# Table buffers, store queues and the low parts of the gate matrices in a hybrid S5 / FNet kernel on Trainium2

## The chip, the cores and the metric

The kernel runs on one core of a Trainium2 chip. The metric is the device time of one execution in microseconds (us), the median over several runs. A core has five engines that run their own instruction lists and wait for each other by semaphores: PE (TensorE, matrix products; PEld is its weight load), DVE (VectorE), ACT (ScalarE), POOL (GpSimd) and SP (SyncE, which here only issues transfers). Transfers between the chip's main memory and the on-chip memory (DMA) are issued from the queue of an engine, here SP's or POOL's, in the order of the program.

## The reference

Two layers over 1024 latent tokens of width 1024, with 256 context tokens ahead of them. All the change lies in layer 0:

```
hl  = rmsnorm(xl) * (1 + scale) + shift                    # scale, shift, gate = silu(c) @ ada_w + ada_b
pl  = hl @ w_in ;  pc = hc @ w_in[:, :768]                 # 768 S5 + 256 FNet + 1024 gate columns
a   = exp(lam * step) ;  B' = ((a - 1) / lam) * B
s_t = a * s_(t-1) + B' u_t                                 # per group of 16 channels, 64 complex states, two directions
y   = Re(C s) + d * u
ya  = gelu(y) * sigmoid(gelu(y) @ glu_w + glu_b) ;  yb = fft2(u) @ f_w
xl  = xl + gate * (([ya, yb] * silu(z)) @ w_out)
```

Layer 1 (pooling, short convolution) and the last norm follow, and the change doesn't touch them.

## The kernel before

**Projections.** `w_in` comes in 16 blocks ("tiles" m) of 128 columns. Each is loaded into a buffer `raw` (four of them, tag `raw`), and split into a high part `whi` (ACT) and a low part `wlo` = raw − whi (DVE or POOL); one tile on PE is 48 matmuls 128x512: per k, high times high, high times low, low times high. `w_split(name)` makes the two parts, `w_take(name)` hands them out, and a `raw` buffer is free for the next load when `wlo` is done. The order of the loads is a fixed list (`w_init`): from tile 8 on it is win(m+1), then four blocks of `in_ada` that the 32 `adaps` matmuls behind tile m read straight from `raw` (`ada_part`).

**S5 tables.** In m = 0 to 5 (S5 columns) a function `fill()` is called from hooks inside the tiles: it makes the next of 24 tables on DVE and lets PE, ACT and the queues finish the table of two calls before. The first twelve (`bl_task`) are B' matrices: DVE writes `bl`, PE transposes it (`pt`), ACT copies the result to `bltw`, POOL's queue stores it in `bltd`. The other twelve (`cl_task`) are C matrices: DVE writes `cl`, which is stored in `cld` by two transfers; PE multiplies it (`pz`), ACT copies to `z`, DVE adds a diagonal (`dg`), and `z` is stored in `zd` for every second table. `cl` has two buffers and `z` has two. The queue for `cld` and `zd` is `self.sq`: SP's at first, POOL's from tile 6 on.

**B' u.** `bl_mm(i)`, i = 0 to 11, multiplies table i with the projected inputs `ub` (PE `vps`, ACT to `va` for i < 6 and `vb` for the rest). Both are loaded from main memory three calls ahead (`bl_load`). The first six calls lie in the hooks of tile 6 (`fx(0, hook0)`, output `fx`, stored in `xd`), the other six behind it. `vb` takes the place of the buffers of the table stage, so its first write waits for their last stores. The buffers `ut`, `utc`, `bltw`, `blt`, `ub`, `fx` share eight places (tag `slot`).

**Scan.** The scan over blocks of eight tokens is done by DVE: `tree(c, l)` over the context, c = 0 on `va`, c = 1 on `vb`; six single steps of `va` (SKEW); then 121 fused steps of six small operations each, kept in `bgq`, which `bg(n)` deals out. They are dealt in the hooks of tile 7 (`fx(1, ...)`) and of the gate tiles m = 8 to 15, so DVE scans while PE multiplies. The low parts of matrices 8 to 15 are made by POOL meanwhile. Behind the scan stands the y phase: `y_copy` (`sy`, ACT and DVE), `y_mm` (`yps`), `y_gelu`, then FNet, GLU, output, layer 1.

The program order is as written, with some reordering by a scheduler; each engine and each queue runs its own list in order.

Of the kernel before, what the change touches and what calls it, by code (L numbers as in the profile page):

```python
# [9 lines left out]
F32 = mybir.dt.float32  # L10
F32R = mybir.dt.float32r
I32 = mybir.dt.int32
AF = mybir.ActivationFunctionType
# [4 lines left out]
P = 128  # L18
# [176 lines left out]
class Builder:  # L195
# [218 lines left out]
    def s5_prelim(self, tp, s5s, raw):  # L414
# [88 lines left out]
                    self.act(self.acf[:, o[0], o[1]], pw[:, k, 8], scale=sc)  # L503
        return tables, inputs

    def bl_task(self, b, hf):

        nc = self.nc
        g4 = slice(8 * b + 4 * hf, 8 * b + 4 * hf + 4)
        bl = self.gt.tile([P, 2, 4, 16, 8], F32, tag="bl", name="bl", bufs=2)  # L510

        def dve():
            p = self.gt.tile([P, 4, 16, 8], F32, tag="blp", name="blp", bufs=1)
            B = [x[:, g4].unsqueeze(3).to_broadcast([P, 4, 16, 8]) for x in (self.bbs, self.bb[:, 0], self.bb[:, 1])]
            W = [self.pwb[:, i, g4].unsqueeze(2).to_broadcast([P, 4, 16, 8]) for i in range(3)]
            self.mul(p, B[0], W[0])
            self.mul(bl[:, 0], B[2], W[2])
            self.mul(bl[:, 1], B[1], W[1])
            self.sub(bl[:, 0], p, bl[:, 0])
            self.add(bl[:, 1], p, bl[:, 1])  # L520

        def pe():
            blt = self.slot("bltw").rearrange("p (r g n) -> p r g n", r=2, g=4)
            for ri in range(2):
                pt = self.ps("m", "pt")
                for g in range(4):
                    nc.tensor.transpose(pt[:, g * P:g * P + P], bl[:, ri, g].rearrange("p h s -> p (h s)"),  # L527
                                        self.c("ident"))
                self.act(blt[:, ri].rearrange("p g n -> p (g n)"), pt)
            nc.gpsimd.dma_start(self.bltd[b][:, :, 4 * hf:4 * hf + 4], blt)  # L530
        return dve, pe

    def cl_task(self, b, hf):
# [1 line left out]
        nc = self.nc  # L535
        g0 = 8 * b + 4 * hf
        g4 = slice(g0, g0 + 4)
        cl = self.kt.tile([P, 2, 4, 144], F32, tag="cl", name="cl", bufs=2)

        def dve():  # L540
            p = self.kt.tile([P, 4 * 144], F32, tag="clp", name="clp", bufs=1)
            p4 = p.rearrange("p (g e h) -> p g e h", g=4, e=9)
            C = [x[:, g4].unsqueeze(2).to_broadcast([P, 4, 9, 16]) for x in (self.cbs, self.cb[:, 0], self.cb[:, 1])]
            W = [self.pwc[:, i, :, g4].rearrange("p e g -> p g e").unsqueeze(3).to_broadcast([P, 4, 9, 16])
                 for i in range(3)]
            c4 = cl.rearrange("p r g (e h) -> p r g e h", e=9)
            self.mul(p4, C[0], W[0])
            self.mul(c4[:, 0], C[2], W[2])
            self.mul(c4[:, 1], C[1], W[1])
            self.sub(c4[:, 0], p4, c4[:, 0])  # L550
            cf = cl[:, 1].rearrange("p g e -> p (g e)")
            self.stt(cf, p, -1.0, cf, ALU.mult, ALU.subtract)
            for d in range(2):
                r = slice(64 * d, 64 * d + 64)
                o = 16 * (1 - d)
                self.sq.dma_start(self.cld[b][r, :, 4 * hf:4 * hf + 4], cl[r, :, :, o:o + 128])

        def pe():
            pz = [self.ps("m", "pz"), self.ps("m", "pz")]
# [188 lines left out]
    def layer0(self, es):  # L748
# [187 lines left out]
        for x in rest:  # L936
            if not isinstance(x, int):
                x()
        tables(0)
        inputs = inputs()  # L940
        for _ in range(4):
            next(inputs)


# [3 lines left out]
            return hh[k], hlo[k]  # L948

        todo = []  # L950
        for b in range(6):
            todo += [(self.bl_task, b, 0), (self.bl_task, b, 1)]
# [5 lines left out]
        self.sq = nc.sync  # L958

        def flush():  # L960
            for b, z in self.zq:
                self.sq.dma_start(self.zd[b].rearrange("a p e -> p a e"), z)
            self.zq = []

        def fill():
            flush()
            if len(pend) == 2 or not todo:
                if pend:
                    pend.pop(0)()
            if todo:  # L970
                f, b, hf = todo.pop(0)
                t = f(b, hf)
                if f == self.cl_task and b + hf == 0:
                    self.add(self.cbs, self.cb[:, 0], self.cb[:, 1])
                t[0]()
                pend.append(t[1])
# [2 lines left out]

        def bl_load(i):  # L980
            b, hf = divmod(i, 2)
            blt = self.slot("blt").rearrange("p (r g n) -> p r g n", r=2, g=4)
            nc.sync.dma_start(blt, self.bltd[b][:, :, 4 * hf:4 * hf + 4])
            ub = self.slot("ub")[:, 0:768].rearrange("p (g j) -> p g j", g=4)
            nc.sync.dma_start(ub, self.ud[b][4 * hf:4 * hf + 4].rearrange("g h s j -> (h s) g j"))
            blq.append((blt, ub))

        for m in range(6):
# [11 lines left out]
            if m == 1:  # L1000
                tables(1)
                sx.close()
                self.gt = ax.enter_context(tc.tile_pool(name="gt", bufs=1))
                self.kt = kx.enter_context(tc.tile_pool(name="kt", bufs=1, side="right"))
# [8 lines left out]
            self.mm3([(pc[:, :TC], 0, TC)], hi, lo, lambda k: (chh[k], chl[k]), 8)  # L1013
            if m == 0:
                self.w_split(names[2])
                for _ in inputs:
                    pass
            else:
                fill()
# [14 lines left out]
        def bl_mm(i):  # L1034
            blt, ub = blq.pop(0)
            for ri in range(2):
                for g0, n in ((0, 3), (3, 1)):
# [7 lines left out]
                    c, gl = divmod(4 * i + g0, NH)  # L1045
                    dst = v[c][:, :, ri, gl:gl + n].rearrange("p i g -> p g i")
                    src = ps[:, 0:160 * n].rearrange("p (g i) -> p g i", g=n)
                    self.act(dst, src)
            if i + 3 < 12:
                bl_load(i + 3)  # L1050

        blk = list(range(12))
        self.sq = nc.gpsimd

        def fx(ct, hook):
            x = self.slot("fx")
# [4 lines left out]
            return lambda: nc.gpsimd.dma_start(xd[:, ct], x)  # L1061

        def hook0(k):
            if k not in (2, 5):
                bl_mm(blk.pop(0))
                fill()

        fx(0, hook0)()
# [53 lines left out]
        while blk:  # L1122
            bl_mm(blk.pop(0))
            if len(blk) == 0:
                self.w_split(names[8], nc.gpsimd)
            if len(blk) < 5:
                tree(0, 4 - len(blk))
        for i in range(NC_, NC_ + SKEW):
# [7 lines left out]
        store = fx(1, lambda k: self.bg(2 if k % 4 else 1))  # L1136
        zt = [self.slot(f"zt{k}") for k in range(KD)]
        gates = [(0, ch) for ch in range(8, 12)] + [(1, ch) for ch in range(12)]
        for m in range(8, 16):
            k = m - 8  # L1140
            hl = self.w_take(names[m])
            if m < 15:
                self.w_split(names[m + 1], nc.gpsimd)
            if m == 8:
                store()
            self.proj(hl, hr, 8, lambda p, c0, c1: self.act(zt[k][:, c0:c1], p, AF.Silu),
                      hook=lambda k: self.bg(2 if k % 4 else 1))
# [678 lines left out]
```

## Time and profile before

| | before |
|---|---|
| time, median of 3 runs | 913.28 us (912.3 to 913.72) |
| the profiled execution: its time / its span | 915.5 us / 913.7 us |
| mean granted TensorE clock | 0.976 |
| busy in the span: PE, DVE, ACT, POOL | 95%, 74%, 38%, 10% |
| DMA moved | 129.16 MB, mean 141 GB/s |

Times in the rows are microseconds from the start of the span of the profiled execution, which is 2.2 us longer than the median of the other runs. A row of a timeline is: start, duration, engine, line, operation, output<-inputs, shape, count, and in brackets the idle time of the engine just before and what ended it. PE is near full almost everywhere; the stretches where it isn't are what a change of order can win.

### The profile page before, as it was taken

Reading aid. Unit: us, or ns where it says so; the run is one execution under the profiler, and the core shown is the slowest. Engines: PE = TensorE matmul, PEld = TensorE weight load, DVE = VectorE, ACT = ScalarE, POOL = GpSimd, SP = SyncE. Lnnn points to the kernel's source line nnn. Section 1 sums busy time; section 2 is a strip of 40 time slices with the busy share of each in tenths; the row PEclk is TensorE's granted clock in tenths of the full one; section 3 lists DMA queues with packets and bytes.
Section 4 is the critical chain, followed back from the end, with each engine's and each line's share of the span. In section 5 each row is a group of like instructions: output and inputs, shape, how many; then the busy total and the mean of one; then the engine's idle time right before and its main releaser. Section 6 shows DMA issues by size and latency. Waiting matters only on the chain.

```text
span 913.7 us, 14101 instructions
## 1 busy us (share of the span) xinstructions
PE 864.6 (95%) x5312; PEld 708.2 (78%) x5312; DVE 673.0 (74%) x1740; ACT 343.4 (38%) x597; POOL 94.2 (10%) x91
## 2 busy tenths in 40 slices
PE   9997998989999967799999999999999999999995
PEld 4666886768777747787888999877778888878995
DVE  7777997857999996755457376698887776785354
ACT  4547341446112109843433143542222333263111
POOL 0002321221221212300016001000000000000000
PEclk9899999999999988999999999999999999999997
DMA  9642779993455565951255303102111111233022
GB/s 349 267 173 74 221 249 268 228 364 128 162 208 190 192 220 157 310 162 54 69 188 179 134 29 93 47 13 74 63 45 50 46 47 56 79 130 151 1 94 93
DMA packets 62212, 129.16 MB, mean 141 GB/s; under 512 B 5760, under 2 KB 32560, under 8 KB 62016
## 3 DMA queue, kind: packets, MB, share of 16 engines
q1 hardware_dynamic: 55280, 104.45, 34.4%
q0 software_dynamic: 6864, 23.81, 8.4%
q8 instruction: 42, 0.69, 0.3%
q14 instruction: 26, 0.21, 0.1%
HBM read 100.03 MB, written 28.21 MB: 140 GB/s over the span
## 4 chain that ended last, share of the span: by engine, by line
PE 64%; DVE 22%; ACT 6%; DMA 5%; issue 1%; SPq 1%; DVEq 0%; POOL 0%; ACTq 0%
PE acc L373 32%; PE acc L1743 19%; DVE va L218 11%; DVE vb L218 2%; DMA ub<-ud 2%; PE acc L883 2%; ACT vb L243 2%; PE yps L1205 1%; DMA mt<-zd 1%; PE pt L527 1%; DVE xt L218 1%; PE rsb L694 1%; PE uc L373 1%; DVE wlo L218 1%; PE pps L1652 1%
## 5 line engine op out<-in xcount | busy, mean ns | idle before, releaser
L373 PE MATMUL acc<-hh,whi 128*128 128x512 f32 (+1 forms) x352 | 113.3, 388 | 3.9 <-ACT whi L243 3.9
L373 PE MATMUL acc<-hl,whi 128*128 128x512 f32 (+1 forms) x352 | 109.9, 379 | 0.0
L373 PE MATMUL acc<-hh,wlo 128*128 128x512 f32 (+1 forms) x352 | 109.4, 377 | 0.0
L373 PEld LDWEIGHTS acc<-hh,whi 128*128 128x128 f32 x352 | 63.6, 192 | 19.3 <-issue 5.1
L373 PEld LDWEIGHTS acc<-hh,wlo 128*128 128x128 f32 x352 | 66.1, 191 | 13.6 <-DVE wlo L218 0.5
L373 PEld LDWEIGHTS acc<-hl,whi 128*128 128x128 f32 x352 | 66.0, 191 | 13.3
L243 ACT ACTIVATE whi<-hh 128x512 fp32r<-128x512 f32 (+4 forms) x44 | 26.9, 629 | 110.4 <-DVE hh L218 97.1
L243 ACT ACTIVATE whi<-raw 128x512 fp32r<-128x512 f32 (+3 forms) x65 | 51.7, 799 | 37.1 <-DMA raw<-in_win 16.7
L1743 PE MATMUL acc<-th,whi 128*128 128x512 f32 x160 | 63.3, 396 | 1.2 <-DVE hl L218 1.2
L218 DVE TENSOR_TENSOR va<-va 128x48 f32<-128x48 f32 (+1 forms) x258 | 62.8, 244 | 0.4
L1743 PE MATMUL acc<-tl,whi 128*128 128x512 f32 x160 | 62.4, 390 | 0.3 <-DVE tl L218 0.3
L1743 PE MATMUL acc<-th,wlo 128*128 128x512 f32 x160 | 62.3, 389 | 0.0
L218 DVE TENSOR_TENSOR wlo<-raw,whi 128x512 fp32r<-128x512 f32 (+3 forms) x57 | 48.4, 854 | 16.5 <-ACT whi L243 16.4
L239 DVE SCALAR_TENSOR_TENSOR xl<-acc,adac,xl 128x256 f32<-128x256 f32 (+1 forms) x48 | 27.3, 570 | 38.5 <-PE acc L373 36.4
L218 DVE TENSOR_TENSOR wlo<-hh,whi 128x512 fp32r<-128x512 f32 (+4 forms) x44 | 30.4, 690 | 24.9 <-ACT whi L243 24.9
L1743 PE MATMUL acc<-hh,whi 128*128 128x512 f32 x120 | 47.5, 396 | 0.0
L1743 PE MATMUL acc<-hh,wlo 128*128 128x512 f32 x120 | 46.8, 390 | 0.3 <-DVE wlo L218 0.3
L1743 PE MATMUL acc<-hl,whi 128*128 128x512 f32 x120 | 46.7, 389 | 0.0
L373 PE MATMUL acc<-th,hl 128*128 128x256 f32 (+1 forms) x144 | 45.9, 319 | 0.5 <-DVE hl L218 0.5
L373 PE MATMUL acc<-th,hh 128*128 128x256 f32 (+1 forms) x144 | 46.3, 321 | 0.1
L373 PE MATMUL acc<-hh,wh 128*128 128x256 f32 (+1 forms) x144 | 46.2, 321 | 0.0
L373 PE MATMUL acc<-hh,wl 128*128 128x256 f32 (+1 forms) x144 | 46.1, 320 | 0.0
(295 smaller groups left out, 2124.0 us busy)
## 6 DMA issues: line engine op xcount, KB each, us to landing
raw<-in_ada SPq DMA_DIRECT2D x44, 512.0 KB, 5.9
raw<-in_win SPq DMA_DIRECT2D x38, 512.0 KB, 3.7
raw<-in_wout SPq DMA_DIRECT2D x16, 512.0 KB, 3.8
bltd<-bltw POOLq DMA_DIRECT2D x12, 512.0 KB, 5.0
blt<-bltd SPq DMA_DIRECT2D x12, 512.0 KB, 7.7
cl<-cld POOLq DMA_DIRECT2D x12, 512.0 KB, 6.5
cld<-cl SPq DMA_DIRECT2D x18, 256.0 KB, 4.9
ub<-ud SPq DMA_DIRECT2D x12, 384.0 KB, 6.9
```

Source lines behind the costliest of these rows:

```text
L218: (eng or self.nc.vector).tensor_tensor(out, a, b, op=op)
L239: self.nc.vector.scalar_tensor_tensor(out, a, s, b, op0=op0, op1=op1)
L243: self.nc.scalar.activation(out, a, func, **kw)
L373: self.nc.tensor.matmul(p, a[:, w], b[:, c0:c1], start=(j == 0 and i == 0), stop=(last and i == 2))
L527: nc.tensor.transpose(pt[:, g * P:g * P + P], bl[:, ri, g].rearrange("p h s -> p (h s)"), self.c("ident"))
L694: self.nc.tensor.matmul(p2[:, P * i:P * i + P], self.ones, dg[:, i], start=True, stop=True)
L883: nc.tensor.matmul(acc[m][h], a[:, w], b[:, 512 * h:512 * h + 512], start=(k == 0 and i == 0), stop=(k == 7 and i == 2))
L1205: nc.tensor.matmul(ps[:, o], sy[:, ri, g], cl[:, ri, g], start=False, stop=(ri == 1))
L1652: nc.tensor.matmul(ps, pwt[:, i], st[i][:, 4 * h:4 * h + 4], start=True, stop=True)
L1743: nc.tensor.matmul(ps, x[:, sl], y, start=bool(new and k == 0 and i == 0), stop=(k == 3 and i == 2), skip_group_check=True)
```

## The change

- bl and cl tables share one set of buffers `tab`: three on the right side and every fourth in the pool `gt` as long as at least five tasks are left; before, two for `bl` in `gt` and two for `cl`. The scratch of both is one tag, `tabp`.
- All stores of `cld` and `zd` are issued from POOL's queue.
- The bl tasks run in the order 3 to 11, 0, 1, 2, and the transposed matrices of tasks 0, 1 and 2 stay on chip: three stores and three loads of 512 KB each go.
- `tables(0)` (six ACT operations, `pwb`) is written behind the split of matrix 2; two of the prepared inputs come ahead instead of four.
- `hook0`: bl_mm at k = 0 to 5 (before 0, 1, 3, 4, 6, 7) and fill at every k but 1 (seven calls, before six).
- The twelve single-group evictions of `vb` go to DVE (COPY); ACT keeps the twelve of three groups.
- The low parts of matrices 8 to 15 are made by DVE. The split of matrix m+1 is written at k = 3 of tile m, before at its head.
- The fused steps are dealt as 13 for each tile (1 at k = 2, 5, 7, else 2); before 14 for each tile and two more behind each `ada_part`.

```diff
+    def tab(self):
+        self.ntab += 1
+        if self.gt is not None and self.ntab % 4 == 0:
+            return self.gt.tile([P, 1152], F32, tag="tab", name="tab", bufs=1)
+        return self.kt.tile([P, 1152], F32, tag="tab", name="tab", bufs=3)
...
-        bl = self.gt.tile([P, 2, 4, 16, 8], F32, tag="bl", name="bl", bufs=2)
+        bl = self.tab()[:, 0:1024].rearrange("p (r g h s) -> p r g h s", r=2, g=4, h=16)
...
+            if 2 * b + hf < 3:
+                self.blts[2 * b + hf] = blt
...
-            nc.gpsimd.dma_start(self.bltd[b][:, :, 4 * hf:4 * hf + 4], blt)
+            if 2 * b + hf > 2:
+                nc.gpsimd.dma_start(self.bltd[b][:, :, 4 * hf:4 * hf + 4], blt)
...
-        cl = self.kt.tile([P, 2, 4, 144], F32, tag="cl", name="cl", bufs=2)
+        cl = self.tab().rearrange("p (r g e) -> p r g e", r=2, g=4)
...
-                self.sq.dma_start(self.cld[b][r, :, 4 * hf:4 * hf + 4], cl[r, :, :, o:o + 128])
+                nc.gpsimd.dma_start(self.cld[b][r, :, 4 * hf:4 * hf + 4], cl[r, :, :, o:o + 128])
...
-        tables(0)
         inputs = inputs()
-        for _ in range(4):
+        for _ in range(2):
             next(inputs)
...
-                self.sq.dma_start(self.zd[b].rearrange("a p e -> p a e"), z)
+                nc.gpsimd.dma_start(self.zd[b].rearrange("a p e -> p a e"), z)
...
+                if len(todo) < 5:
+                    self.gt = None
...
                 self.w_split(names[2])
+                tables(0)
...
-                    self.act(dst, src)
+                    if n == 1 and i > 5:
+                        nc.vector.tensor_copy(dst, src)
+                    else:
+                        self.act(dst, src)
...
-            if k not in (2, 5):
+            if k < 6:
                 bl_mm(blk.pop(0))
+            if k != 1:
                 fill()
...
-                self.w_split(names[8], nc.gpsimd)
+                self.w_split(names[8])
...
+        def steps(k):
+            self.bg(1 if k in (2, 5, 7) else 2)
+
+        store = fx(1, steps)
...
-            if m < 15:
-                self.w_split(names[m + 1], nc.gpsimd)
...
-                      hook=lambda k: self.bg(2 if k % 4 else 1))
+            def hook(k):
+                if k == 3 and m < 15:
+                    self.w_split(names[m + 1])
+                steps(k)
...
-                self.bg(2)
```

What the order of the instructions becomes at three places follows; the rows have no times.

The first is SP's queue around tiles 4 to 6: `cld` and `zd` are the stores of the table stage (lines L556 and L962), `blt` and `ub` the loads for bl_mm, `raw` a weight load. This is the middle of that list before:

```order
L556 DMA cld_85<-cl 128x4x128 x2
L983 DMA blt<-bltd_79 128x2x512
L985 DMA ub<-ud_97 128x4x192
L323 DMA raw<-in_ada 128x1024
L962 DMA zd_90<-z 128x2x240
L556 DMA cld_86<-cl 128x4x128 x4
L962 DMA zd_91<-z 128x2x240
L556 DMA cld_87<-cl 128x4x128 x4
L962 DMA zd_92<-z 128x2x240
```

And this is POOL's list of the same tables now (`ud` are the projected inputs of tiles 4 and 5, `tab` a shared table buffer):

```order
L567 DMA cld_84<-tab 128x4x128 x4
L567 DMA cld_85<-tab 128x4x128 x4
L1037 DMA ud_100<-ut 1024x1x128
L1040 DMA ud_100<-utc 1024x1x32
L1041 DMA ud_100<-utc 1024x1x32
L972 DMA zd_90<-z 128x2x240
L567 DMA cld_86<-tab 128x4x128 x4
L972 DMA zd_91<-z 128x2x240
L567 DMA cld_87<-tab 128x4x128 x4
```

The stores have left SP's queue, where they stood between loads, and the first `zd` store now stands on POOL's behind eight `cld` stores and three `ud` stores.

The second is DVE's list where the last `vb` evictions are, between the parts of tree(0); rows with + are new, rows with − were there before:

```order
 L218 TENSOR_TENSOR va<-va,tr 128x4x48 x2
-L218 TENSOR_TENSOR tr<-va,acf_2136 128x96 x2
+L1065 COPY vb<-vps 128x160 x2
+L218 TENSOR_TENSOR tr<-va,acf_2127 128x96 x2
 L218 TENSOR_TENSOR va<-va,tr 128x2x48 x2
-L218 TENSOR_TENSOR tr<-va,acf_2137 128x48 x2
+L1065 COPY vb<-vps 128x160 x2
+L218 TENSOR_TENSOR wlo<-raw,whi 128x1024
+L218 TENSOR_TENSOR tr<-va,acf_2128 128x48 x2
 L218 TENSOR_TENSOR va<-va,tr 128x48 x2
 L218 TENSOR_TENSOR va<-va,acf 128x96
```

The copies of the last two bl_mm and the low part of matrix 8 now stand ahead of the last level of tree(0), of the six single steps (the last row is their first operation) and of tree(1).

The third is SP's queue in the gate stage. Its loads are the same as before, one `in_win` and four `in_ada` for each tile, but some wait for another engine. Before, for tiles from 12 on:

```order
L323 DMA raw<-in_win 128x1024 [waits DMAHW6_49,DMAHW2_49,PE_49]
L323 DMA raw<-in_ada 128x1024 [waits DMAHW3_49,PE_49]
L323 DMA raw<-in_ada 128x1024 [waits DMAHW4_49,PE_49]
L323 DMA raw<-in_ada 128x1024 [waits DMAHW5_49,PE_49]
L323 DMA raw<-in_ada 128x1024 [waits DMAHW6_49,Pool_49]
```

Now, from the first loads of the stage (the `in_win` rows here are matrices 10 and 11):

```order
L323 DMA raw<-in_ada 128x1024 [waits DMAHW4_49,DVE_49]
L323 DMA raw<-in_ada 128x1024 [waits DMAHW5_49,DMAHW2_49,PE_49]
L323 DMA raw<-in_win 128x1024 [waits DMAHW6_49,DMAHW3_49,PE_49]
L323 DMA raw<-in_ada 128x1024 [waits DMAHW1_49,DVE_49]
L323 DMA raw<-in_ada 128x1024 [waits DMAHW4_49,PE_49]
L323 DMA raw<-in_ada 128x1024 [waits DMAHW5_49,PE_49]
L323 DMA raw<-in_ada 128x1024 [waits DMAHW6_49,DVE_49]
L323 DMA raw<-in_win 128x1024 [waits DMAHW7_49,PE_49]
```

The wait of one `in_ada` load for POOL, which had made `wlo`, has become a wait for DVE, which makes it now among its scan steps.

## Rows read from the trace of the kernel before

**Rows 1.** Stretches: length, busy PE, PEld, DVE, ACT, POOL, granted clock, DMA share, GB/s.

```profile
145.00:165.00 20.00, 16.36 (x144) 11.68 (x143) 13.01 (x24) 2.10 (x8) 0.00 (x0) 0.83 1.00 296
185.00:205.00 20.00, 17.55 (x242) 14.68 (x242) 10.49 (x38) 9.06 (x19) 3.95 (x6) 1.00 1.05 372
232.00:334.00 102.00, 102.00 (x627) 75.78 (x625) 102.00 (x647) 17.92 (x39) 19.57 (x13) 1.00 0.61 210
334.00:346.70 12.70, 0.43 (x4) 0.23 (x2) 12.64 (x82) 2.52 (x4) 0.00 (x0) 0.66 0.20 62
```

**Rows 2.** Waits of PE, 60 to 380 us: sum, times, longest.

```profile
PE yps L1205 <- ACT sy L243: 12.3, 1, 12.3
PE acc L373 <- ACT whi L243: 3.9, 1, 3.9
```

**Rows 3.** Waits of DVE, 130 to 220 us; then ACT's timeline.

```profile
DVE cl L218 <- DMA cld<-cl: 12.4, 5, 5.4
...
162.22 0.76 ACT L243 ACTIVATE z<-pz 128x128 f32<-128x128 f32 x4 [13.79 <-DMA zd<-z]
```

**Rows 4.** SP's queue, timeline: start, time in the queue.

```profile
155.67 0.43 SPq L962 DMA_DIRECT2D zd<-z  x1
...
208.48 0.36 SPq L985 DMA_DIRECT2D ub<-ud  x1
```

**Rows 5.** DMA issues, 85 to 220 us: KB each, median us to landing.

```profile
cld<-cl SPq DMA_DIRECT2D x18, 256.0 KB, 4.9
...
cld<-cl POOLq DMA_DIRECT2D x6, 256.0 KB, 7.6
...
zd<-z POOLq DMA_DIRECT2D x3, 240.0 KB, 7.3
xd<-fx POOLq DMA_DIRECT2D x1, 512.0 KB, 6.5
```

**Rows 6.** PE's timeline: in tile 5, at tile 6, first and last adaps.

```profile
153.81 1.22 PE L373 MATMUL acc<-hh,whi 128*128 128x512 f32 x2
...
167.72 0.74 PE L373 MATMUL acc<-hh,whi 128*128 128x512 f32 x2
...
238.81 1.94 PE L588 MATMUL adaps<-raw,cond 128*32 128x256 f32 x32
...
332.07 1.94 PE L588 MATMUL adaps<-raw,cond 128*32 128x256 f32 x32
```

**Rows 7.** ACT's timeline: outputs of tile 6, then the vb evictions.

```profile
200.49 1.12 ACT L243 ACTIVATE fx<-acc 128x512 f32<-128x512 f32 x2
204.65 13.57 ACT L243 ACTIVATE vb<-vps 128x480 f32<-128x480 f32 x24 [3.04 <-DMA ub<-ud]
218.01 1.07 ACT L243 ACTIVATE whi<-raw 128x1024 fp32r<-128x1024 f32 x1
```

**Rows 8.** DVE's timeline: a wlo of the table stage, then trees and scan.

```profile
147.01 1.22 DVE L218 TENSOR_TENSOR wlo<-raw,whi 128x1024 fp32r<-128x1024 f32 x1
...
218.26 1.83 DVE L218 TENSOR_TENSOR tr<-vb,acf 128x768 f32<-128x768 f32 x2 [4.05 <-ACT vb L243]
...
229.16 0.25 DVE L218 TENSOR_TENSOR va<-va,acf 128x96 f32<-128x96 f32 x1
...
229.62 2.43 DVE L218 TENSOR_TENSOR va<-va,vb 128x48 f32<-128x48 f32 x1
...
232.21 0.25 DVE L218 TENSOR_TENSOR va<-va,acf 128x96 f32<-128x96 f32 x1
...
233.03 0.25 DVE L218 TENSOR_TENSOR va<-va,acf 128x96 f32<-128x96 f32 x1
```

**Rows 9.** POOL's timeline: a wlo in the scan.

```profile
229.59 2.40 POOL L218 TENSOR_TENSOR wlo<-raw,whi 128x1024 fp32r<-128x1024 f32 x1 [7.25 <-ACT whi L243]
```

**Rows 10.** ACT's timeline: the first copies of the y phase.

```profile
344.53 6.50 ACT L243 ACTIVATE sy<-va 64x512 f32<-64x512 f32 x6 [10.07 <-DVE va L218]
```

**Rows 11.** The head, DVE's timeline: the first table.

```profile
89.81 0.69 DVE L218 TENSOR_TENSOR blp<-bbs,pwb 128x512 f32<-128x512 f32 x1 [1.27 <-ACT acf L243]
```

More of the change, by code (lines that the diff above doesn't have):

```diff
@@ L509, in bl_task @@
         g4 = slice(8 * b + 4 * hf, 8 * b + 4 * hf + 4)
-        bl = self.gt.tile([P, 2, 4, 16, 8], F32, tag="bl", name="bl", bufs=2)
+        bl = self.tab()[:, 0:1024].rearrange("p (r g h s) -> p r g h s", r=2, g=4, h=16)
         def dve():
-            p = self.gt.tile([P, 4, 16, 8], F32, tag="blp", name="blp", bufs=1)
+            p = self.kt.tile([P, 576], F32, tag="tabp", name="blp", bufs=1)[:, 0:512]
+            p = p.rearrange("p (g h s) -> p g h s", g=4, h=16)
             B = [x[:, g4].unsqueeze(3).to_broadcast([P, 4, 16, 8]) for x in (self.bbs, self.bb[:, 0], self.bb[:, 1])]
@@ L537, in cl_task @@
         g4 = slice(g0, g0 + 4)
-        cl = self.kt.tile([P, 2, 4, 144], F32, tag="cl", name="cl", bufs=2)
+        cl = self.tab().rearrange("p (r g e) -> p r g e", r=2, g=4)
         def dve():
-            p = self.kt.tile([P, 4 * 144], F32, tag="clp", name="clp", bufs=1)
+            p = self.kt.tile([P, 576], F32, tag="tabp", name="clp", bufs=1)
             p4 = p.rearrange("p (g e h) -> p g e h", g=4, e=9)
@@ L950, in layer0 @@
         todo = []
-        for b in range(6):
-            todo += [(self.bl_task, b, 0), (self.bl_task, b, 1)]
+        for i in (3, 4, 5, 6, 7, 8, 9, 10, 11, 0, 1, 2):
+            todo.append((self.bl_task, *divmod(i, 2)))
         for b in range(6):
@@ L957, in layer0 @@
         self.zq = []
-        self.sq = nc.sync
+        self.blts = {}
         def flush():
             for b, z in self.zq:
-                self.sq.dma_start(self.zd[b].rearrange("a p e -> p a e"), z)
+                nc.gpsimd.dma_start(self.zd[b].rearrange("a p e -> p a e"), z)
             self.zq = []
@@ L981, in bl_load @@
             b, hf = divmod(i, 2)
-            blt = self.slot("blt").rearrange("p (r g n) -> p r g n", r=2, g=4)
-            nc.sync.dma_start(blt, self.bltd[b][:, :, 4 * hf:4 * hf + 4])
+            blt = self.blts.pop(i, None)
+            if blt is None:
+                blt = self.slot("blt").rearrange("p (r g n) -> p r g n", r=2, g=4)
+                nc.sync.dma_start(blt, self.bltd[b][:, :, 4 * hf:4 * hf + 4])
             ub = self.slot("ub")[:, 0:768].rearrange("p (g j) -> p g j", g=4)
@@ L1003, in layer0 @@
                 self.gt = ax.enter_context(tc.tile_pool(name="gt", bufs=1))
+                self.ntab = 0
                 self.kt = kx.enter_context(tc.tile_pool(name="kt", bufs=1, side="right"))
@@ L1052, in layer0 @@
         blk = list(range(12))
-        self.sq = nc.gpsimd
         def fx(ct, hook):
@@ L1134, in layer0 @@
         rest = [step((1, i)) for i in range(n - SKEW, n)]
-        store = fx(1, lambda k: self.bg(2 if k % 4 else 1))
+        def steps(k):
+            self.bg(1 if k in (2, 5, 7) else 2)
+        store = fx(1, steps)
         zt = [self.slot(f"zt{k}") for k in range(KD)]
@@ L1141, in layer0 @@
             hl = self.w_take(names[m])
-            if m < 15:
-                self.w_split(names[m + 1], nc.gpsimd)
             if m == 8:
                 store()
-            self.proj(hl, hr, 8, lambda p, c0, c1: self.act(zt[k][:, c0:c1], p, AF.Silu),
-                      hook=lambda k: self.bg(2 if k % 4 else 1))
+            def hook(k):
+                if k == 3 and m < 15:
+                    self.w_split(names[m + 1])
+                steps(k)
+            self.proj(hl, hr, 8, lambda p, c0, c1: self.act(zt[k][:, c0:c1], p, AF.Silu), hook=hook)
             for l, ch in gates[2 * k:2 * k + 2] if k < 7 else ():
                 self.ada_part(l, ch)
-                self.bg(2)
             if k == 4:
```

## The prediction

> **What bounds the kernel now.** I read the windows first, then PE's waits, then back along the engine that ended each wait. The windows [rows 1] show four kinds of stretch. In 145–165 PE works 16.36 of 20 us at a mean granted clock of 0.83 and DVE only 13.01: somebody waits for something else. In 185–205 PE lacks 2.45 us while DMA stands at a share of 1.05 and 372 GB/s. In 232–334 PE and DVE are both full, 102 of 102. In 334–346.7 PE does 0.43 us and DVE 12.64: here DVE's scan alone sets the end, and PE's largest wait, 12.3 us for `sy`, says the same [rows 2]. `sy` starts on ACT at 344.53, released by the scan [rows 10], and from there ACT, PE and DVE feed each other without a gap as large. So the question for the whole change is: **at what time does the scan end, and is PE done with the gate tiles by then?** PE finishes its last `adaps` at 332.07 + 1.94 = 334.0 [rows 6], 10.5 us ahead of the scan.
>
> The scan's own sum closes. It starts at 229.16 [rows 8], a fused step lasts 233.03 − 232.21 = 0.82 us, 121 steps are 99.8 us, and the rest to 344.53 is 15.6 us. That is seven times 2.2: while POOL makes a `wlo` (2.40 us, [rows 9]), one DVE operation that otherwise takes 0.20 takes 2.43 [rows 8]. The start in turn hangs on `vb`: its evictions run 204.65 to 218.0 [rows 7], DVE waits 4.05 us for them, then tree(1) takes 10.9 us to 229.16, with one such block of about 2.1 in it [rows 8].
>
> **Low parts on DVE.** A `wlo` costs DVE 1.22 us (1.14 from start to start) [rows 8] instead of a block of 2.2. Seven in the scan: 15.6 − 8.0 = 7.6 us less; the eighth frees tree(1) of 2.1 and is paid by 1.14 ahead of it.
>
> **Order at the start of the scan.** Before, DVE went through all of tree(0) and the six single steps while it would have waited for `vb` anyway. By the order shown, the last copies and `wlo` of matrix 8 now stand ahead of the last level of tree(0), the six single steps and tree(1). Call the end of the vb evictions V. Then come ACT's `whi` 1.07 [rows 7], `wlo` 1.14, the last tree level 0.7 and six single steps at about 0.78, 4.7 (estimates: a fused step of six operations is 0.82 and a single one of three, each waiting for the one before, is near that), and tree(1) 10.9 − 2.1 = 8.8: the scan starts at V + 16.4. Before it was 229.16 − 218.0 = V + 11.2. So **5.2 us that lay under the wait for vb now lie on the path.** The cover that is gone is the waiting itself.
>
> **Table stage.** Before, DVE waits 12.4 us, in five waits, for a `cld` store to free one of two `cl` buffers, and ACT waits 13.79 us for a `zd` store to free `z` [rows 3]; that store, issued at 155.67 [rows 4], stood in SP's list behind `cld` stores that themselves waited for tables. Three or four buffers end the first kind: a table takes DVE about 3.7 us (12.4 of waits taken off), so a buffer is wanted again after some 11, and a store lands in 7.6 from POOL's queue against 4.9 from SP's [rows 5]. The wait for `z` stays but moves. On POOL's list the first `zd` stands behind eight `cld` and three `ud` stores; I estimate its issue at about 149.5 (the fourth table without waits ends near 145.5, and five issues follow), so it lands 7.3 later [rows 5], at 156.8, where ACT went on at 162.22 [rows 3]: 5.4 us earlier. With the waits behind it tile 6 starts about 6 us earlier: 161.7 instead of 167.72 [rows 6]. The bounds are 0 (the store is no earlier) and 7.0 (all that DVE lacks in 145–165).
>
> **Tile 6 and vb.** Before, tile 6 runs from 167.72 until ACT takes its output at 200.49, 32.8 us, of which PE lacks 2.45 [rows 1] and ACT is late by about 1.1. One more `pz` (0.7) is inside now. 32.8 − 2.45 − 1.1 + 0.7 = 29.9: the output is taken at 191.6 and copied by 192.7. The load of the tenth `ub` (the last but one) needs the place of `fx`, so it waits for the store of `fx` in `xd`, 6.5 us [rows 5]: issue at 199.5 where the last `ub` was issued at 208.48 [rows 4]. It lands some 5.4 us later (estimate: 218.0 − 208.48 less the bl_mm and evictions behind it), and two bl_mm of 2.2 and an eviction of 0.6 follow: **V ≈ 209.9**, 8.1 earlier. The twelve small evictions moved to DVE take ACT off the path here (24 evictions took 13.57 us [rows 7]; twelve large ones need less than the time the loads leave), and the last `zd` store, issued about 12 us before the output of tile 6 now, no longer sets the start. The three matrices kept on chip take 3 MB off the queues; I give them nothing beyond the 2.45 us.
>
> **Into the gate tiles.** The scan starts at 209.9 + 16.4 = 226.3 (2.9 earlier). DVE alone would end it at 226.3 + 99.8 + 8.0 = 334.1. But `wlo` of matrix 9 now stands behind 18 steps (13 dealt in tile 7, five in tile 8): 226.3 + 14.9 + 1.2 = 242.4. PE wants it after tile 7, tile 8 and an `adaps` block, two tiles of 11.4 and 1.94: the period is (332.07 − 238.81) / 7 = 13.32 [rows 6], so about 209 + 24.7 = 233.7. **PE stands for nearly 9 us** and then runs at the lower of its clock levels (1.2 of 2.4 GHz) for a while (after a stall a pair of matmuls took 1.22 against 0.74 [rows 6]; the 0.83 of 145–165, two stalls in 20 us, bounds that at 1.7 us for each). Worse, `raw` of matrix m+1 is now held until DVE comes to its `wlo`, so the fourth `in_ada` block of tiles 8 and 9 is loaded only when the first `adaps` has freed a place: some 4 us more at the end of tile 9 (at tile 8 it hides under the wait for `wlo`). Tile 10 then starts near 260.3, tile 11 at 275, the others every 13.3: tile 15 at about 328, end 339.2, last `adaps` 341.1. From tile 10 on DVE is tied to PE: win(m+1) is loaded after the `adaps` ahead of tile m, so `wlo` of 15 can't end before about 4.2 us into tile 14 (load 3.7 less what lies before the tile, `whi` 1.07, `wlo` 1.14), 318.8; 25 steps, 20.6, stand behind it. The scan ends at **339.4**, 5.1 us before 344.53. PE, done at 341.1, needs the first `sy` at 341.6 by the same distance as before: both ends meet.
>
> **Head.** `tables(0)` behind the split ends PE's wait of 3.9 us for `whi` [rows 2]. But the first table's first operation waits for `acf` [rows 11], and ACT's work ahead of `acf` is the same sum, so PE reaches the first transpose 4 us earlier and waits there for the table. I give it 0; bounds 0.8 lost (a longer idle time, so more at the lower clock) to 2 gained.
>
> **Sum.** 8.1 (V) − 5.2 (order) + 7.6 (wlo) − 5.4 (DVE tied to PE, 339.4 against 334.1) = 5.1 us, on the profiled execution 915.5 to 910.4; on the median of the runs, 2.2 lower, 913.28 to about **908.2**.
>
> **A rule against the moved stores.** A `cld` store takes 7.6 us from POOL's queue and 4.9 from SP's [rows 5], in part because the former fell into the fuller stretch. The Trainium skill, page "SBUF — State Buffer", section "SBUF: two separate sides", says that GpSimd can't write the descriptors of its DMAs while VectorE holds the port pair both share, and advises the other queues for such transfers. By it the stores would be late whenever DVE is busy with that kind of operation; by the row they are 2.7 us later, which the third buffer hides.
>
> **Rivals.**
> 1. *The tie to PE doesn't bite*: SP loads ahead enough that DVE runs free. For it: DVE has 1.3 us to spare in each tile (13.3 − 13 × 0.82 − 1.14). Against: the order of waits on SP. Then the scan ends at 334.1, PE's own end must come to 336, time 903.
> 2. *The stores on one queue are late* (the other side): POOL issues 24 `cld`, 6 `zd` and the `ud` stores in order while DVE is busy. If a `zd` lands no earlier than 162.2, the 6 us at tile 6 go and V is about 216–218. The order of the scan then decides: the time is 913.28 − (218.0 − V) + 3.0, so slower for V above 215; at 217, 915.3. For it: DMA was at a share of 1.05 in 185–205 and the bl_mm loads now come at a shorter distance. The port rule above would do the same.
> 3. *PE becomes the last*: if the stall at tile 9 or the late fourth block costs 2 to 4 us more, the last `adaps` ends at 343 to 345 and the time is 910 to 912.
>
> Chances: forecast 0.42 (own range 905.5 to 910), rival 1 0.20, rival 2 0.20, rival 3 0.18. The range leaves out the corners, V at 218 at the top and rival 1 with an earlier V at the bottom: 901.8 to 914.8. A difference of 0.2%, 1.8 us, is about what separates two medians here from no change. Faster by more: the forecast, rival 1 and over half of rival 3, 0.72; within: 0.14; slower, most of rival 2: 0.14.
>
> **What would show it.** DVE's waits for `cld` gone, one wait of ACT for `zd` near 157, tile 6 from about 162, V near 210, no 2.4 us operation in the scan, a wait of PE for `wlo` of about 9 us near 234 with a lower clock behind it, waits of PE for `raw` in `adaps`, short waits of DVE for `whi` in every gate tile, scan end near 339, a wait of PE for `sy` of a us or two. If V is above 215, or DVE never waits in the gates, the sum is wrong at that term.

## The result: slower by 1.1%, mostly through one wait that the sum didn't have

The changed kernel takes 923.69 us (median of 4, 921.54 to 925.98) against 913.5 for the kernel before: a ratio of 1.011, 95% interval 1.0084 to 1.0136. The forecast was 908.2, range 901.8 to 914.8: wrong in sign and by 15.5 us. The profiled execution took 925.98 us, span 924.1.

PE's waits of the changed kernel, 60 to 400 us (sum, times, longest), say where the time is; of before see [rows 2]:

```profile
PE vps L1058 <- DMA ub<-ud: 15.4, 2, 14.2
PE adaps L599 <- DMA raw<-in_ada: 5.7, 2, 3.0
PE pt L537 <- issue: 5.1, 1, 5.1
PE acc L373 <- DVE wlo L218: 4.3, 1, 4.3
...
PE yps L1229 <- ACT sy L243: 2.1, 1, 2.1
```

The windows (columns as in [rows 1]) show the same stretches:

```profile
145.00:165.00 20.00, 18.08 (x206) 13.15 (x206) 15.99 (x31) 3.82 (x12) 10.05 (x13) 1.00 0.78 192
165.00:185.00 20.00, 12.45 (x172) 9.66 (x168) 12.94 (x24) 7.79 (x16) 10.09 (x13) 0.91 0.90 236
185.00:205.00 20.00, 13.31 (x186) 11.15 (x193) 4.15 (x9) 6.91 (x15) 2.20 (x3) 0.75 0.77 240
232.00:334.00 102.00, 91.93 (x522) 68.25 (x521) 96.45 (x609) 19.03 (x39) 1.31 (x2) 0.97 0.46 162
```

145–165 improved as forecast: PE 18.08 us against 16.36 and the granted clock back at 1.00. The loss is in 165–205: PE works 25.8 of 40 us, where it worked 37.2 before (17.55 in 185–205 [rows 1], and here the window ahead of it in the kernel before):

```profile
165.00:185.00 20.00, 19.68 (x272) 15.53 (x271) 18.51 (x35) 10.08 (x23) 5.87 (x8) 1.00 0.88 219
```

The gate stage has idle time of PE now, 10 of 102 us.

One wait of 14.24 us, on the timeline of PE, is most of it; the loads that it waits for are SP's (start, time in the queue):

```profile
191.69 0.50 PE L1058 MATMUL vps<-ub,blt 128*64 128x160 f32 x1 [14.24 <-DMA ub<-ud]
```

```profile
171.03 0.64 SPq L997 DMA_DIRECT2D blt<-bltd  x1
171.76 1.90 SPq L999 DMA_DIRECT2D ub<-ud  x1
173.80 1.81 SPq L997 DMA_DIRECT2D blt<-bltd  x1
175.66 1.75 SPq L999 DMA_DIRECT2D ub<-ud  x1
177.51 8.57 SPq L997 DMA_DIRECT2D blt<-bltd  x1
```

These are the loads of bl_mm(3), (4) and (5). Issued at 171.0, the first `blt` takes 12.8 us to land (6.5 in the kernel before), its `ub` 19.8, the next `blt` 19.0; the third stands 8.57 us in the queue. In the same time POOL's queue moves stores:

```profile
170.30 1.50 POOL L567 DMA_DIRECT2D cld<-tab  x2 [2.06 <-DVE tab L239]
171.79 0.90 POOL L1037 DMA_DIRECT2D ud<-ut  x1
172.60 0.97 POOL L1040 DMA_DIRECT2D ud<-utc  x1
173.38 1.06 POOL L1041 DMA_DIRECT2D ud<-utc  x1
174.55 1.53 POOL L567 DMA_DIRECT2D cld<-tab  x2
```

The `ud` stores of tile 5 had left at 165.5 to 169.8 before, ahead of the loads (the first of these was issued at 177.97):

```profile
165.48 0.85 POOL L1021 DMA_DIRECT2D ud<-ut  x1 [20.93 <-ACT ut L243]
169.04 0.85 POOL L1024 DMA_DIRECT2D ud<-utc  x1 [2.71 <-ACT utc L243]
169.81 0.95 POOL L1025 DMA_DIRECT2D ud<-utc  x1
```

Now they stand behind `cld` stores, whose table is ready only at 169.4.

Most of what lies behind this wait went as the prediction had it, some 14.5 us later. The rows that answer to [rows 3, 7, 8, 10] (timelines of ACT and DVE, one fence each; the last PE row is the wait for `wlo` of matrix 9):

```profile
157.80 0.76 ACT L243 ACTIVATE z<-pz 128x128 f32<-128x128 f32 x4 [9.87 <-DMA zd<-z]
...
208.31 1.09 ACT L243 ACTIVATE fx<-acc 128x512 f32<-128x512 f32 x2 [2.14 <-PE acc L373]
...
224.48 1.07 ACT L243 ACTIVATE whi<-raw 128x1024 fp32r<-128x1024 f32 x1
...
355.66 6.50 ACT L243 ACTIVATE sy<-va 64x512 f32<-64x512 f32 x6
```

```profile
223.94 0.46 DVE L1065 COPY vb<-vps 128x160 f32<-128x160 f32 x1 [0.65 <-PE vps L1059]
225.59 1.22 DVE L218 TENSOR_TENSOR wlo<-raw,whi 128x1024 fp32r<-128x1024 f32 x1 [1.19 <-ACT whi L243]
...
232.02 1.82 DVE L218 TENSOR_TENSOR tr<-vb,acf 128x768 f32<-128x768 f32 x2
...
240.72 0.25 DVE L218 TENSOR_TENSOR va<-va,acf 128x96 f32<-128x96 f32 x1
```

```profile
256.82 1.22 PE L373 MATMUL acc<-hh,wlo 128*128 128x512 f32 x2 [4.35 <-DVE wlo L218]
...
353.38 1.94 PE L599 MATMUL adaps<-raw,cond 128*32 128x256 f32 x32
```

vb ends at 224.5 instead of the forecast 209.9 (V, counted here and below to the start of ACT's `whi` of matrix 8, as the forecast counted it before: 218.0); `fx` is taken at 208.3 instead of 191.6.

### The profile page after: what moved, and what is told of

Same layout as the page of the kernel before. It is cut to its first block, busy times and chain, and to the rows that moved or that the text cites. A ratio compares the mean times of both kernels' runs of the same rounds, so it can differ in the third digit from the quotient of the medians.

```text
span 924.1 us, 14085 instructions
## 1 busy us (share of the span) xinstructions
PE 861.9 (93%) x5312; PEld 706.6 (76%) x5312; DVE 667.4 (72%) x1760; ACT 340.7 (37%) x585; POOL 87.8 (10%) x101
## 4 chain that ended last, share of the span: by engine, by line
PE 76%; DVE 10%; DMA 6%; ACT 6%; issue 2%; POOL 0%; SPq 0%; DVEq 0%; ACTq 0%; POOLq 0%
PE acc L373 41%; PE acc L1767 19%; DMA ub<-ud 3%; DVE va L218 2%; PE adaps L599 2%; PE vps L1058 2%; PE acc L894 2%; PE yps L1229 1%; DMA zd<-z 1%; PE pt L537 1%; DMA mt<-zd 1%; DVE xt L218 1%; DVE wlo L218 1%; PE uc L373 1%; ACT sy L243 1%
## 5 line engine op out<-in xcount | busy, mean ns | idle before, releaser
L373 PE MATMUL acc<-hh,whi 128*128 128x512 f32 (+1 forms) x352 | 113.3, 388 | 0.0
L218 DVE TENSOR_TENSOR wlo<-raw,whi 128x512 fp32r<-128x512 f32 (+3 forms) x65 | 58.1, 898 | 19.2 <-ACT whi L243 19.1
L218 DVE TENSOR_TENSOR va<-va 128x48 f32<-128x48 f32 (+1 forms) x258 | 53.6, 209 | 0.4
```

Of the source, the lines that this page charges most:

```text
L218: (eng or self.nc.vector).tensor_tensor(out, a, b, op=op)
L373: self.nc.tensor.matmul(p, a[:, w], b[:, c0:c1], start=(j == 0 and i == 0), stop=(last and i == 2))
```

## The experiments

Theory A: the stores that now all go through POOL's queue hold the first loads of bl_mm back. Rivals: B, the loads are simply asked for too soon; C, stores and loads together are too much from whatever queue; and the gate half as the cause. The kernel before was run beside each group; its medians there were 914.0, 915.0, 914.3 and 914.8 us, so the ratios compare better than the times.

| kernel | time, us | ratio to before, 95% interval |
|---|---|---|
| the change | 923.69 | 1.0110 [1.0084, 1.0136] |
| 1 cld and zd stores back | 915.69 | 1.0013 [0.9992, 1.0034] |
| 2 ud stores on ACT's queue | 920.05 | 1.0059 [1.0034, 1.0084] |
| 3 gate half back | 922.89 | 1.0097 [1.0061, 1.0133] |
| 4 gate half alone | 915.95 | 1.0013 [0.9995, 1.0031] |
| 5 hooks of tile 6 back | 922.06 | 1.0097 [1.0064, 1.0130] |
| 6 cld, zd stores on ACT's queue | 939.06 | 1.0268 [1.0236, 1.0299] |
| 7 as 1, vb and wlo of 8 back | 911.82 | 0.9968 [0.9951, 0.9984] |
| 8 cld stores back | 916.49 | 1.0021 [0.9994, 1.0048] |
| 9 short rows of tile 5 moved | 919.71 | 1.0053 [1.0032, 1.0073] |
| 10 bl_mm's loads on POOL's queue | 921.60 | 1.0075 [1.0047, 1.0102] |
| 11 as 7, gate half back | 913.09 | 0.9980 [0.9962, 0.9997] |
| 12 as 7, split at k = 0 | 910.74 | 0.9954 [0.9932, 0.9976] |
| 13 as 8, ud of tile 5 late | 916.56 | 1.0015 [0.9995, 1.0035] |
| 14 as 9, again | 920.93 | 1.0076 [1.0048, 1.0104] |

**1. Stores back** (all others below that start from "the change" differ from it only as shown).

```diff
-                nc.gpsimd.dma_start(self.cld[b][r, :, 4 * hf:4 * hf + 4], cl[r, :, :, o:o + 128])
+                self.sq.dma_start(self.cld[b][r, :, 4 * hf:4 * hf + 4], cl[r, :, :, o:o + 128])
...
-                nc.gpsimd.dma_start(self.zd[b].rearrange("a p e -> p a e"), z)
+                self.sq.dma_start(self.zd[b].rearrange("a p e -> p a e"), z)
```

> The changed kernel with one part undone: cld and zd stores go where they went before (SP's queue until tile 6, then POOL's). Theory A, the stores that now all stand on POOL's queue reach the DMA engines together with the first loads of bl_mm and make these land after 13 to 20 us: PE's wait for ub at bl_mm(3), 14.2 us now, falls below 4 us, and the time is 911 to 916. Theory B, the first loads are late whatever queue the stores use, since three matrices kept on chip and bl_mm at every k call for the next loads too soon: the wait stays above 10 us and the time at 920 to 925.

915.69 us; the wait for `ub` is one of 2.6 us, the first `blt` lands in 6.5 us. A holds, B is out as the whole cause. V is 213.1, 11.4 us earlier than in the changed kernel and still 3.2 later than forecast: tile 6 lasts 33.7 us here, from the first row to the second.

```profile
161.55 0.73 PE L373 MATMUL acc<-hh,whi 128*128 128x512 f32 x2
```

```profile
195.22 1.08 ACT L243 ACTIVATE fx<-acc 128x512 f32<-128x512 f32 x2 [2.14 <-PE acc L373]
```

**2. ud stores from ACT's queue.**

```diff
-            nc.gpsimd.dma_start(um[:, :, 32:160], ut.rearrange("p (s j) -> p s j", s=8))
+            nc.scalar.dma_start(um[:, :, 32:160], ut.rearrange("p (s j) -> p s j", s=8))
```

(and the same for the two `uc` stores)

> The changed kernel with one more change: the stores of the projected inputs (ud, three for each tile) leave from ACT's queue, so that those of tile 5 no longer stand behind cld stores on POOL's list. Theory A1, it is these late stores of short rows, issued at 171.8 to 174.4 just when the loads start, that slow the loads: they leave near 160 and 164, the wait at bl_mm(3) falls below 5 us, time 911 to 915. Theory A2, it is the cld and zd stores themselves: the wait stays above 9 us, time 918 to 925. ACT pays some 0.5 us for each of 18 issues, under 1 us in sum on the path.

920.05 us: the time is as A2 has it, the wait as A1 has it. In the profiled execution the wait for `ub` is 1.1 us and the first `blt` lands in 8.7, with the `cld` stores still on POOL's queue; but that execution (917.3 us) was 2.7 us below the median, and ACT costs time of its own (3.1 us of PE's waits for `va`). So the late `ud` stores are a part of the loss, and going by the time not the whole.

**3. Gate half back**, and **4. gate half alone** (on the kernel before):

```diff
-                self.w_split(names[8])
+                self.w_split(names[8], nc.gpsimd)
...
-            def hook(k):
-                if k == 3 and m < 15:
-                    self.w_split(names[m + 1])
-                steps(k)
+            if m < 15:
+                self.w_split(names[m + 1], nc.gpsimd)
```

(3, with the old dealing of steps; 4 is the reverse on the kernel before)

> The changed kernel with the gate half undone: low parts of matrices 8 to 15 on POOL, split at the head of the tile, steps dealt as before. The wait at bl_mm(3) stays (12 to 16 us). From the end of the vb evictions to the first sy copy the kernel before took 126.5 us and the changed one 131.3: if that difference is the gate half, the time falls by 4.8 us to about 919. If the tie of DVE to PE in the gates cost nothing and the loss is all ahead of vb, it stays within 1.5 us of 923.7.

> The kernel before with the gate half alone (low parts by DVE, split at k = 3, 13 steps for each tile). vb ends as before near 218. By the terms of the prediction it loses 5.2 us of order, gains 7.6 on low parts and loses 5.4 or so on the tie to PE: 916 to 919, with no 2.4 us operation left in the scan, a wait of PE for wlo of matrix 9 of 6 to 9 us and scan end near 348. Rival: DVE runs free in the gates, and it is 3 us faster than before, 910.5.

3 gives 922.89 us: the gate half is not the loss. (The wait for `ub` was shorter than expected, 9.6 us at the longest, in an execution 2.2 us below the median.) It did not give back 4.8 us either, and its profile shows one reason: the copies of vb on DVE still stand ahead of tree(0)'s last level and the six steps, so the scan again starts late, 18.0 us behind vb, now with two blocks by POOL's `wlo` in it. 4 gives 915.95, 0.13% above before, at the lower edge of what was expected and with an interval that holds no change. In its profile the scan starts 16.2 us behind V (11.2 before), and from there to `sy` it takes 112.4 us (115.4 before): 5.0 lost, 3.0 won. PE's wait for `wlo` is 4.2 us, not 6 to 9. One of the two edits, `wlo` of 8 on DVE or the copies on DVE, is enough to expose the six steps.

**5. Hooks back.**

```diff
-            if k < 6:
+            if k not in (2, 5):
                 bl_mm(blk.pop(0))
-            if k != 1:
                 fill()
```

> The changed kernel with the hooks of tile 6 as before: bl_mm at k = 0, 1, 3, 4, 6, 7 and six fills. Theory B, bl_mm(3) comes too soon for its loads: asking for it about 4 us later takes its wait from 14 to under 6 us and the time falls by 6 to 8 us, to 916 to 918. Theory A, the loads share the DMA engines with stores from POOL's queue and are starved: the wait falls by 4 us at most and the time by 0 to 4 us, 919.5 to 923.7, since what PE gains there it gives up later.

922.06 us, with waits for `ub` of 10.8 us in sum, the longest 8.8: the wait fell by more than A has it and by less than B has it. The first three `blt` still land in 11.0, 17.4 and 16.2 us. Asking later shortens the wait, and gives little of the time back: B is out.

**6. Stores from ACT's queue.**

```diff
-                nc.gpsimd.dma_start(self.cld[b][r, :, 4 * hf:4 * hf + 4], cl[r, :, :, o:o + 128])
+                nc.scalar.dma_start(self.cld[b][r, :, 4 * hf:4 * hf + 4], cl[r, :, :, o:o + 128])
```

(and the same for `zd`)

> The changed kernel with the cld and zd stores issued from ACT's queue, whose transfers are of the hardware kind as SP's; their place in the program is the same, the ud stores stay on POOL's queue. Theory A, it is the POOL queue's transfers that take the DMA engines from SP's loads: the wait for ub at bl_mm(3) is under 4 us, blt lands in 7 to 10 us, time 913 to 918 (ACT waits for tables before it issues, some of which it has to spare). Theory C, it is only that stores and loads now meet at the same time, from whatever queue: blt still lands in 12 to 19 us, wait over 8, time 919 to 925.

939.06 us, above both expectations, and it decides nothing: ACT stands still before each pair of `cld` issues until DVE has made the table, 5 us and more each time, and PE behind it; the first load of bl_mm(3) leaves only at 188.1, so loads and stores hardly meet (DMA share 0.53 in 165–185). ACT's timeline:

```profile
183.60 1.28 ACTq L567 DMA_DIRECT2D cld<-tab  x2
184.99 0.39 ACT L243 ACTIVATE utc<-uc 128x256 f32<-128x256 f32 x1 [5.24 <-issue]
```

**7. Order** (on 1).

```diff
-                    if n == 1 and i > 5:
-                        nc.vector.tensor_copy(dst, src)
-                    else:
-                        self.act(dst, src)
+                    self.act(dst, src)
...
-                self.w_split(names[8])
+                self.w_split(names[8], nc.gpsimd)
```

> The first experiment's kernel (cld and zd stores where they went before) with the vb evictions all on ACT again and the low part of matrix 8 on POOL again, so that tree(0) and the six single steps stand under the wait for vb as before. If these two edits put 5.2 us on the path, as the prediction has it, the scan starts 11 to 12 us behind the last vb eviction instead of 16.4, the wait of PE for the low part of matrix 9 is under 1 us, and the time falls by 3.4 to 5.2 us from 915.7, to 910.5 to 912.3. If the gate stage is set by PE and the raw buffers anyway, it stays at 914.5 to 916.

911.82 us, 0.32% below before. V is 213.2 and the scan starts at 224.35, 11.2 us behind it as before, where experiment 1 has 16.2; PE waits for no `wlo`. So 5.0 of the 5.2 us of the order are shown, and 3.9 of them (0.45% by the ratios) arrive at the end. ACT's timeline, then DVE's:

```profile
213.20 1.07 ACT L243 ACTIVATE whi<-raw 128x1024 fp32r<-128x1024 f32 x1
```

```profile
213.45 1.83 DVE L218 TENSOR_TENSOR tr<-vb,acf 128x768 f32<-128x768 f32 x2 [3.37 <-ACT vb L243]
...
224.35 0.25 DVE L218 TENSOR_TENSOR va<-va,acf 128x96 f32<-128x96 f32 x1
```

**8. cld stores back** (as 1, with `zd` left on POOL's queue).

> The changed kernel with the cld stores alone where they went before; the zd stores stay on POOL's queue. If it is the 24 cld stores (6 MB) that starve the loads, this is as good as the first experiment, 914 to 917, with a wait at bl_mm(3) under 4 us. If the six zd stores (1.4 MB in rows of 960 bytes) do it, it stays at 920 to 924. In between, 917 to 920, if it is the sum of bytes.

916.49 us, as good as 1: it is the `cld` stores, not `zd`. What each queue moved in 165 to 190 us (q0 is POOL's, q1 SP's: packets, MB, share of the 16 engines' time), first in the changed kernel, then here:

```profile
q0 software_dynamic: 1123, 3.61, 55.4%
q1 hardware_dynamic: 1869, 2.64, 35.0%
```

```profile
q1 hardware_dynamic: 6345, 6.11, 79.0%
q0 software_dynamic: 515, 1.61, 20.1%
```

SP's queue, which has all loads, moves 2.64 MB in the changed kernel and 6.11 here (four `cld` stores, 1.0 MB, among them), in the same 25 us; the engines are busy 0.91 and 1.00 of it. POOL's packets are 3.2 and 3.1 KB on average, SP's 1.4 and 1.0.

More than the queue differs, though: here the stores stand ahead of the loads in SP's own list, and while the first loads run, from 171 to 178 us, POOL's queue moves nothing:

```profile
q1 hardware_dynamic: 1795, 2.04, 97.9%
```

In the changed kernel both queues have work from 174 to 184 us, and POOL's takes over two thirds of the engines' time:

```profile
q0 software_dynamic: 561, 1.85, 69.8%
q1 hardware_dynamic: 757, 0.99, 32.0%
```

So 1 and 8 show that the first loads lose when the `cld` stores meet them; they don't show that it matters from which queue a store comes (rival C).

**9, 14. Short rows of tile 5 moved to tile 0** (the profile is 14's).

```diff
-            nc.gpsimd.dma_start(um[:, :, 0:32], uc)
-            nc.gpsimd.dma_start(um[:, :, 160:192], uc)
+            for d in ((0, 5), (1,), (2,), (3,), (4,), ())[m]:
+                ud = self.ud[d].rearrange("g h s j -> (g h) s j")
+                nc.gpsimd.dma_start(ud[:, :, 0:32], uc)
+                nc.gpsimd.dma_start(ud[:, :, 160:192], uc)
```

> The changed kernel with the two short-row stores of tile 5 (the context columns in ud, 1024 rows of 128 bytes each) taken out of their place at 172.6 to 174.4 us: tile 0 stores its own context columns there instead, at 85 us, so the context columns of the last tile are wrong, with the same count of transfers. Theory A1, these short rows meet the first loads and hold the DMA engines: the loads of bl_mm(3) land in under 10 us, the wait falls below 4 us, time 914 to 917. Theory A2, it is the cld stores on POOL's queue: the wait stays above 8 us, time 919.5 to 923.7.

> The same kernel as the one with the two short-row stores of tile 5 moved to tile 0 (919.7 us), for its profile. Half of the loss is gone there, so the wait at bl_mm(3) should be 4 to 10 us, with blt landing in 8 to 13 us, against 14.2 and 12.8 to 19 in the changed kernel and 2.4 in the kernel with cld stores as before.

919.71 and 920.93 us: 3 to 5 us of the loss by the ratios. `blt` lands in 10.8 to 11.9 us, the longest wait for `ub` is 7.0. The two transfers, 0.26 MB of the stretch's 3.6 on that queue, cost more than their bytes, but half of the loss or more stays.

**10. Loads on POOL's queue.**

```diff
-                nc.sync.dma_start(blt, self.bltd[b][:, :, 4 * hf:4 * hf + 4])
+                nc.gpsimd.dma_start(blt, self.bltd[b][:, :, 4 * hf:4 * hf + 4])
...
-            nc.sync.dma_start(ub, self.ud[b][4 * hf:4 * hf + 4].rearrange("g h s j -> (h s) g j"))
+            (nc.gpsimd if i > 2 else nc.sync).dma_start(ub, self.ud[b][4 * hf:4 * hf + 4].rearrange("g h s j -> (h s) g j"))
```

> The changed kernel with the loads of bl_mm (blt always, ub from the fourth on) issued from POOL's queue too, behind the stores that stand ahead of them in the program, so that loads and stores share one queue in order. Theory A, loads from SP's queue get less of the DMA engines than stores from POOL's: now the loads have the same right, land in 6 to 10 us from issue, the wait at bl_mm(3) is under 5 us, time 913 to 918. Theory C, stores and loads together are more than the engines move in that stretch, from whatever queue: loads still land in 12 us and more, the wait is over 8 us, time 920 and up.

921.60 us: mixed. In order with the stores the loads land in 9.4 to 9.9 us, not 12.8 to 19, as A has it, and the engines move more in the same 25 us (7.13 MB against 6.28); against C's "still 12 us". But `ub` of bl_mm(3) is issued 3.1 us later (counted from the start of tile 6), behind stores that wait for their tables, so PE still waits 7.3 us and the time hardly falls.

```profile
q0 software_dynamic: 1919, 6.57, 87.3%
q1 hardware_dynamic: 144, 0.52, 7.8%
...
blt<-bltd POOLq DMA_DIRECT2D x4, 512.0 KB, 9.6
```

**11. Gate half back on 7**, and **12. split at k = 0 on 7** (11 as in 3):

```diff
-                if k == 3 and m < 15:
+                if k == 0 and m < 15:
```

> The order experiment (911.8, 3 us faster than before on its chip) with the gate half undone too: low parts by POOL, split at the head, steps dealt as before. What is left of the change is the shared table buffers, the three matrices kept on chip, the hooks of tile 6 and the order in the head. If low parts on DVE bring next to nothing, since DVE is tied to PE there (1.2 us from vb to the first sy copy), it stays at 911 to 913; if they bring the 7.6 us less blocking that the prediction counts, it goes up to 916 to 919.

> The order experiment with the split of matrix m+1 written at k = 0 of tile m, not k = 3: DVE makes each low part five steps earlier, so the raw buffers come free 4 us earlier. If the waits of PE for raw in adaps (6.4 us in two) and the tie of DVE to PE come from the late low parts, the waits fall to under 3 us and the time to 908 to 910. If DVE then only waits for whi, since the load of win(m+1) itself comes late, the time stays within 1 us of 911.8 or rises.

11 gives 913.09 us (0.9980), 7 gave 0.9968: low parts on DVE are worth about 0.1%, with intervals that overlap. 12 gives 910.74 us (0.9954), the fastest of all; one wait for `raw` of 5.1 us is left in the gates, not under 3 as expected, and the step from 7 is within the intervals.

**13. ud stores of tile 5 held back** (on 8).

```diff
+            if m < 5:
+                late()
...
+            if k == 1:
+                late()
```

(`late()` holds the three ud stores of the tile.)

> The kernel of the cld experiment (cld stores where they went before, 916.5 us) with the three ud stores of tile 5 alone held back to where they stand in the changed kernel, among the first loads of bl_mm. If these stores by themselves delay the loads, the wait at bl_mm(3) rises from 2.4 us to 6 us and more and the time by 3 to 5 us, to 919 to 922. If it takes the cld stores on POOL's queue as well, the time stays at 916 to 917.5.

916.56 us, no slower than 8, though in its profile one `ub` lands after 14.5 us and PE waits 8.1 us for `ub` in four waits. Late `ud` stores do harm in another way here: one `blt` can't be issued for 6.9 us, since a `ud` store that hasn't landed still holds its place in `slot` (SP's waits):

```profile
SPq L998 <- DMA ud<-ut: 6.9, 1, 6.9
```

Without the `cld` stores on POOL's queue the late `ud` stores cost next to nothing of the time.

## Why the prediction was wrong, step by step

- **Waits for `cld` and `zd` in the table stage: right.** DVE's wait for `cld` is gone; the first `zd` is issued at 150.0 (149.5) and ACT goes on at 157.8 (156.8); tile 6 starts at 162.7 (161.7).
- **"Tile 6 and vb": the step that failed.** It took off all 2.45 us that PE lacked there and let tile 6 last 29.9 us, as if the loads of bl_mm kept landing as before: what the moved stores do to these loads stood in the sum at nothing. Its output came at 208.3, 16.7 us late, and V at 224.5, 14.6 late. With the stores back V came at 213.1 (1), so 11.4 us of this are the stores; the other 3.2 are the credit for tile 6 itself, which lasted 33.7 us in 1, 33.2 in 8, 34.5 in 7 and 32.4 in 12, so hardly less than the 32.8 before in any of them. Why it didn't get shorter stays open. Rival 2 had the right place and side and the wrong object: not a late `zd` (it was in time) but late loads on SP's queue, at up to 19.8 us. The prediction had noted the full DMA share and a shorter distance for the loads there, and priced neither; its range, up to 914.8, left out even the upper half of rival 2 (V at 217 is 915.3 by its own formula). What ran: `cld` stores on POOL's queue (about 8 us of the loss go with them: experiments 1 and 8), with the `ud` stores that they hold up as an addition (3 to 5 of these: 2, 9 and 14) that costs next to nothing alone (13).
- **V to scan, 16.4 us: 16.2 measured** (224.5 to 240.7). Before it was 11.2; experiment 7 brought the 11.2 back.
- **`wlo` of matrix 9 at 16.1 us after the scan's start: right** (256.8). PE's stall was 2.8 for `raw` and 4.35 for `wlo`, 7.1, not 9, since the late `raw` block of tile 8 didn't hide under the wait but came ahead of it.
- **Gates tied to PE: right.** Last `adaps` ends 114.6 us after the scan's start (114.8), the scan 113.3 (113.1), and DVE waits 5.2 us for `whi` in the gates, where the sum took 5.4; four waits, though, and not one in every tile.
- **`sy` with the scan's end: off by 1.7.** On ACT the copy of an `adaps` row, which waits for the last `adaps`, stands ahead; the first `sy` copy came at 355.66, not at 353.99.
- **Head: 0, right.** The wait of 3.9 us for `whi` became one of 5.1 at the first transpose, and the tiles behind are level with before.
- **Low parts on DVE:** 7.6 less blocking and 5.4 given back at the tie: 2.2 net in the sum, 3.0 from scan start to `sy` in experiment 4, about 1 us in 7 against 11, whose intervals overlap.
- **The port rule** that the prediction took from the Trainium skill (page "SBUF — State Buffer", section "SBUF: two separate sides") isn't shown to explain the loss: `cld` stores landed late too (12.8 us at the worst), but so did SP's loads, on which that rule says nothing, and POOL's issues took 0.75 us each as before.

With V at the measured 224.5, the prediction's own later steps give 9.5 us slower than before; 10.2 was measured. With V at 213.1, as in experiment 1, they give 1.9 us faster; 1.2 slower was measured, with an interval that holds no change. So even without the late loads the change as built wins nothing that these runs show: the order of the scan (7) takes back what the table stage gave.

Why loads get so little beside the stores is not settled. 10 speaks for the queue: with loads and stores in one list the loads land in 9.4 to 9.9 us, but they are also issued later. 8 doesn't separate the queue from the meeting, and 6 decided nothing, so C isn't excluded. The Trainium skill, page "DMA: Bandwidth & Descriptors", section "Queues, rings and completion order", says that a DMA engine takes turns between queues by whole packets. With packets of 3.3 KB against 1.3 in 174 to 184 us that would favour POOL's queue, and 1.85 against 0.99 MB agrees in direction, but no run changed the packet size alone.

## What to carry to other kernels

Stores that are off the critical path aren't free: before moving them to another queue, look which loads will be in flight then, and how much each queue moves in that stretch. A store behind a late one on a queue becomes late too; here that brought tile 5's stores into the loads. And an operation added to an engine's list should stand behind the work that hides under the wait, not ahead of it: with that put right and the stores back (experiments 7 and 12) the kernel was 0.3 to 0.5% faster than before.

## What the runs showed of the hardware

The first three of the 512 KB loads in tile 6 landed in 6.5, 9.1 and 12.3 us (experiment 1) and 5.6, 7.7 and 11.2 (8) with POOL's queue idle as they began, in 9.4, 9.9 and 9.8 from POOL's own queue behind its stores (10), and in 12.8, 19.0 and 17.8 from SP's queue beside POOL's stores (the change). In 25 us the engines moved 6.28 MB at a share of 0.91 in the changed kernel and 7.77 MB at 1.00 in experiment 8. By the share alone it would be 6.9: a busy share is not yet a rate.
